# A gated MLP by seven block products in place of eight, with its inner features and residual kept in DRAM between its two halves

## The chip, the cores and the metric

The kernel runs on one core of one Trainium2 chip. Its time is device microseconds of one launch. Below, PE is TensorE (the matmul engine), PEld its weight loads, DVE is VectorE, ACT ScalarE, POOL GpSimd, and SP SyncE, which here only issues DMAs. SBUF is the on-chip memory, PSUM the memory that matmuls write and accumulate in, DRAM the chip's large memory.

## The reference, cut to what matters

Two transformer blocks run one after the other on 1024 tokens of 1024 features in float32. The change concerns the end of the first block: the second norm, the gated MLP with 2816 inner features, and the residual.

```
h = h + m @ w_o                                  # output of the mixer
hn = rms_norm(h, norm2_g)
gate, up = jnp.split(hn @ w_gate_up, 2, axis=-1) # w_gate_up [1024, 2 * 2816]
h = h + (jax.nn.silu(gate) * up) @ w_down        # w_down [2816, 1024]
x = rms_norm(h, final_g)                         # goes into the second block
```

Every float32 product is made of three passes: a matrix X is split into a high part hi(X), rounded to the format that PE multiplies in one pass, and a low part lo(X) = X - hi(X); then X @ Y = hi hi + hi lo + lo hi. So each product of 128 x 128 by 128 x 512 is three matmuls, and each operand costs one copy (ACT) and one subtraction.

## The kernel before, in words

The program is one stream with an order written out by hand: each engine gets its instructions in the order of the Python text, and waits only on semaphores. Tiles come from pools with a fixed number of buffers; a tile that takes over a buffer waits until the last reader of the old one is done. `Side` objects (class Side) are generators whose steps are put between the matmuls of the main stream; `tick` pays them out by an estimate of matmul time.

`Weights` streams the weights: SP loads a raw unit (`wraw`, 3 buffers), ACT makes the high part, POOL the low part (`whi`, `wlo`, 4 buffers each), two units ahead of use. PSUM has 6 banks named `mm` and 2 named `ax`, 128 x 512 each.

In the stage "wo" (line 1047) eight row tiles of h are loaded from x by ACT's queue (L1051), and `add_rows` adds the mixer's output, four column blocks of 256: first columns 0 and 1 for all rows, then the memory of the second block (`mem_steps`, `mem_kv`), then columns 2 and 3 for rows 0 to 3 and for rows 4 to 7. `norm2_steps` norms the first four row tiles beside the matmuls of the last four.

In the stage "mlp" (line 1164) POOL first fills a small table `G` of relative biases (L1175, 32 tiny instructions into an `ev` tile) and stores it 128-fold to DRAM (L1179). Then the normed rows are turned (`n2T`, `to_cols`) into nh, nl: features on partitions, 1024 tokens along the row. For each of 22 tiles of 128 inner features, `gate_up` makes the gate and the up product (8 blocks of K, three matmuls each, two halves of 512 tokens), Silu on ACT, the product of the two on DVE, and the high and low part of the inner feature (`acth`, `actl`). After each group of two or four tiles `down_unit` multiplies them by the rows of w_down and adds the PSUM sum to h in SBUF (L1206); so h gathers six partial sums, and the down product lies between the gate and up products. At the end `final_steps` norm h twice, rows 0 to 3 beside the last down products, rows 4 to 7 beside the first products of the stage "z", which turns rows 0 to 3 first.

Of the kernel before, what the change touches and what calls it, by code (L numbers as in the profile page):

```python
# [58 lines left out]
class Weights:  # L59
    """Streams weights in the order of use: DMA ahead, then exact high and low parts."""  # L60
# [21 lines left out]
    def split_to(self, n, low=None):  # L82
        nc = self.nc
        while self.ns < min(n, len(self.plan)):
# [27 lines left out]
def build(tc, A, out, dbg=None, stop=None):  # L112
# [85 lines left out]
    order = []                      # ("gu", tile) and ("dn", group), as they run
    for gi, (f0, nf) in enumerate(ff_groups):
        for f in range(f0, f0 + nf):  # L200
            order.append(("gu", f))
            if gi and f == f0:
                order.append(("dn", gi - 1))
    order.append(("dn", len(ff_groups) - 1))
    for kind, a in order:
        if kind == "gu":            # gate and up columns of one hidden tile share a unit
            for k0 in (0, 4):
                plan.append(("gu", [cols(wgu, a * 128, 128, k0), cols(wgu, DFF + a * 128, 128, k0)],
                             4, 256))
        else:  # L210
            f0, nf = ff_groups[a]
            for j in range(2):
                for k0 in range(0, nf, 2):
                    plan.append(("dn", cols(wdn, 512 * j, 512, f0 + k0, 2), 2, 512))
# [1471 lines left out]
```

## Time and profile before

| | |
|---|---|
| median of 3 runs | 2272.94 us (2271.72 to 2275.72) |
| the profiled execution: span from first to last instruction | 2270.9 us |
| PE busy | 2225.0 us, 98% |
| PEld busy | 1932.2 us, 85% |
| DVE busy | 1099.9 us, 48% |
| POOL busy | 704.1 us, 31% |
| ACT busy | 676.8 us, 30% |
| mean granted TensorE clock | 0.996 of 2.4 GHz |
| stage "wo" to the first turn of "mlp" | about 985 to 1085 us |
| gated MLP with the down product | about 1085 to 1834 us |

The profile is one execution; all its times are microseconds from the start of the span unless marked ns. A row of the timeline gives start, duration, engine, line, operation, the tile written and the tiles read, and in brackets the idle time before it and what ended that. The duration of a matmul overlaps with the next one, so the spacing of starts is what a matmul costs, not its duration. A row of the groups by line gives count, busy time and the mean of one in ns. A line of the stretches gives, for each engine, busy time and instruction count, then the granted clock, the share of the 16 DMA engines, and GB/s.

### The profile page before, as it was taken

The page shows a single profiled execution, that of the slowest core. Times are in us where ns is not written, and L with a number is a line of the kernel's source. Part 1 is how long each engine was busy: PE and PEld are TensorE (multiplying, and loading weights), DVE is VectorE, ACT ScalarE, POOL GpSimd, SP SyncE. Part 2 cuts the span into 40 slices and gives each one's busy share as a digit, 9 for nine tenths or more (in the row PEclk, how much of TensorE's full clock was granted, in tenths as well). Part 3 has the DMA queues.
Part 4 walks back from the last instruction along what each step waited for, and adds up shares of the span by engine and source line. Part 5 has one row for each costly group of instructions (what it writes and reads, how often), then busy time and mean ns, then how long its engine had stood idle before and what let it go on. Part 6 is the DMA issues. An engine that isn't in the chain of part 4 may idle for free.

```text
span 2270.9 us, 30698 instructions
## 1 busy us (share of the span) xinstructions
PE 2225.0 (98%) x12299; PEld 1932.2 (85%) x12299; DVE 1099.9 (48%) x2327; ACT 676.8 (30%) x1290; POOL 704.1 (31%) x581
## 2 busy tenths in 40 slices
PE   7999999999999999999799999999999999999998
PEld 7789888998888888899788888888888899988998
DVE  6688899888893887332320110101011170831724
ACT  4573211111122876212311112021211252322631
POOL 0213322325542311643243223232322212671121
PEclk9999999999999999999999999999999999999999
DMA  4212122113320000451221111111111132110014
GB/s 145 70 66 75 61 75 70 56 38 112 111 75 25 15 1 22 155 186 60 48 84 40 44 56 38 56 38 56 47 47 56 38 112 71 48 57 19 1 60 146
DMA packets 131950, 146.25 MB, mean 64 GB/s; under 512 B 11200, under 2 KB 112292, under 8 KB 131808
## 3 DMA queue, kind: packets, MB, share of 16 engines
q1 hardware_dynamic: 117600, 103.56, 14.8%
q0 software_dynamic: 8800, 27.54, 3.5%
q10 hardware_dynamic: 5408, 13.20, 1.5%
q8 instruction: 96, 1.57, 0.3%
q14 instruction: 46, 0.38, 0.1%
HBM read 122.48 MB, written 21.76 MB: 64 GB/s over the span
## 4 chain that ended last, share of the span: by engine, by line
PE 88%; DVE 5%; issue 3%; DMA 2%; ACT 1%; POOL 1%; ACTq 0%; DVEq 0%; SPq 0%; POOLq 0%
PE mm L293 26%; PE mm L295 26%; PE mm L294 25%; PE mm L966 2%; PE ax L293 2%; DMA gd<-ev 1%; PE ax L295 1%; PE ax L294 1%; PE ax L1569 1%; PE mm L1511 1%; PE mm L347 1%; DVE scores L575 1%; PE mm L1547 1%; DVE av L1373 1%; PE mm L569 0%
## 5 line engine op out<-in xcount | busy, mean ns | idle before, releaser
L91 POOL TENSOR_TENSOR wlo<-wraw,whi 128x1024 fp32r<-128x1024 f32 (+1 forms) x174 | 416.8, 2415 | 699.0 <-ACT whi L90 679.5
L293 PE MATMUL mm<-nh,whi 128*128 128x512 f32 (+1 forms) x736 | 282.6, 384 | 0.0
L295 PE MATMUL mm<-nh,wlo 128*128 128x512 f32 (+1 forms) x736 | 281.4, 382 | 0.0
L294 PE MATMUL mm<-nl,whi 128*128 128x512 f32 (+1 forms) x736 | 278.8, 379 | 0.0
L90 ACT ACTIVATE whi<-wraw 128x1024 fp32r<-128x1024 f32 (+1 forms) x176 | 178.8, 1050 | 311.3 <-issue 176.9
L295 PE MATMUL mm<-xh,wlo 128*128 128x512 f32 (+2 forms) x736 | 269.9, 367 | 0.0
L294 PE MATMUL mm<-xl,whi 128*128 128x512 f32 (+2 forms) x736 | 269.5, 366 | 0.0
L293 PE MATMUL mm<-xh,whi 128*128 128x512 f32 (+2 forms) x736 | 269.0, 365 | 0.0
L1191 DVE TENSOR_TENSOR ev<-mm,ev 128x512 f32<-128x512 f32 (+1 forms) x46 | 30.7, 668 | 450.3 <-PE mm L295 428.0
L618 DVE MAX8 m<-scores 128x8 f32<-128x272 f32 (+6 forms) x224 | 188.8, 843 | 6.4 <-POOL scores L580 0.2
L620 DVE MATCH_REPLACE8 scores<-m,scores 128x272 f32<-128x272 f32 (+6 forms) x224 | 185.0, 826 | 0.0
L322 POOL TENSOR_TENSOR actl<-ev,acth 128x512 fp32r<-128x512 f32 (+1 forms) x46 | 57.4, 1248 | 356.5 <-ACT acth L1193 356.5
L295 PEld LDWEIGHTS mm<-nh,wlo 128*128 128x128 f32 x736 | 138.2, 188 | 29.2
L294 PEld LDWEIGHTS mm<-nl,whi 128*128 128x128 f32 x736 | 138.1, 188 | 28.3
L293 PEld LDWEIGHTS mm<-nh,whi 128*128 128x128 f32 x736 | 138.3, 188 | 25.4
L294 PEld LDWEIGHTS mm<-xl,whi 128*128 128x128 f32 x736 | 138.5, 188 | 20.5
L293 PEld LDWEIGHTS mm<-xh,whi 128*128 128x128 f32 x736 | 138.3, 188 | 20.3
L295 PEld LDWEIGHTS mm<-xh,wlo 128*128 128x128 f32 x736 | 138.3, 188 | 19.6
L1206 DVE TENSOR_TENSOR h<-mm,h 128x512 f32<-128x512 f32 x96 | 66.3, 692 | 163.5 <-PE mm L295 163.5
L293 PE MATMUL mm<-whi,acth 128*128 128x512 f32 (+1 forms) x368 | 143.7, 391 | 0.0
L295 PE MATMUL mm<-whi,actl 128*128 128x512 f32 (+1 forms) x368 | 143.7, 391 | 0.0
L294 PE MATMUL mm<-wlo,acth 128*128 128x512 f32 (+1 forms) x368 | 143.7, 390 | 0.0
(320 smaller groups left out, 4833.8 us busy)
## 6 DMA issues: line engine op xcount, KB each, us to landing
wraw<-in_w_in_dram SPq DMA_DIRECT2D x68, 512.0 KB, 3.6
wraw<-in_w_gate_up_dram SPq DMA_DIRECT2D x88, 256.0 KB, 3.3
wraw<-in_w_down_dram SPq DMA_DIRECT2D x22, 512.0 KB, 3.6
mpart<-ev POOLq DMA_DIRECT2D x32, 256.0 KB, 2.3
ev<-mpart POOLq DMA_DIRECT2D x32, 256.0 KB, 3.7
xr<-in_x_dram SPq DMA_DIRECT2D x8, 512.0 KB, 6.6
g1d<-ev ACTq DMA_DIRECT2D x16, 256.0 KB, 2.0
wraw<-in_w_b_dram SPq DMA_DIRECT2D x8, 512.0 KB, 3.3
```

What stands on the lines that cost most here:

```text
L90: nc.scalar.activation(hi[:, :nk * w], r, AF.Copy)
L91: (low or nc.gpsimd).tensor_tensor(lo[:, :nk * w], r, hi[:, :nk * w].bitcast(F32), op=ALU.subtract)
L293: nc.tensor.matmul(o, sh, mh, start=start, stop=False)
L294: nc.tensor.matmul(o, sh, ml, start=False, stop=False)
L295: nc.tensor.matmul(o, sl, mh, start=False, stop=stop)
L322: (eng or nc.gpsimd).tensor_tensor(out_lo, src, hi.bitcast(F32), op=ALU.subtract)
L347: nc.tensor.transpose(tp[:, k * 128:k * 128 + P], r[:, kk * 128:(kk + 1) * 128], ident[:P, :P])
L618: nc.vector.max(m8, s)
L620: nc.vector.match_replace(out=s, in_to_replace=m8, in_values=s, imm_value=TAKEN)
L966: nc.tensor.transpose(tp[:P, h * 128:(h + 1) * 128], lgs[h][:, k0:k0 + P], ident)
L1191: nc.vector.tensor_tensor(g, ou, g, op=ALU.mult)
L1206: nc.vector.tensor_tensor(hs, o, hs, op=ALU.add)
```

## The change

The product of two matrices, each cut into 2 x 2 blocks, takes eight block products. The changed kernel takes seven, with the sums of blocks by Strassen and Winograd (numbered 1 to 7 in the code), for the gate, the up and the down product alike.

For gate and up, the turned rows are cut into two halves of tokens and two halves of K, and seven operands `TM[1]` to `TM[7]` are made once: 1 and 2 are blocks, the others differences of the normed rows, taken before the turn (`turn4`, through the two `ax` banks). A unit is 256 columns of gate or up; per unit DVE makes three sums of weight blocks and later a fourth (`gu_sums`, `gu_prep`), ACT and POOL split each of the seven weight operands, seven products of 12 matmuls run in the order 1, 6, 2, 5, 7, 3, 4 in four banks, and `gu_out`, `block` add the results up; POOL multiplies by the gate. Products 2, 3 and 4 add on to the banks of 1, 5 and 7 after those have been read. At each pair of units POOL makes the seven left operands of the down product (`hidden_sums`), and SP stores them to DRAM (`hd`).

The residual h is stored to DRAM (`hres`) after the mixer and loaded again at the down product. That starts when all inner features are done: seven products over 11 pairs of inner tiles, all of K summed in PSUM, in the order 1, 7, 2, 4, 5, 6, 3; each step loads one operand of the inner features (`ra`) and one or two blocks of w_down, makes the sum for products 7, 4 and 5 on DVE, and splits both operands: ACT copies, POOL's low part for the weights, DVE's for the inner features. Steps are prepared three ahead. The last three steps of each product go row tile by row tile, and `dn_out` adds the result to the blocks of h that take it.

Also moved: `G` is made at the start of "wo" into a tile of its own, the keys and values of the memory go through DRAM, rows 4 to 7 are final before rows 0 to 3, and the high and low weight parts share one ring of eight (`wpart`).

```diff
+    def raw_tile(self):
+        return self.pool.tile([128, 1024], F32, name="wraw", bufs=3)
+    def part_tile(self):
+        return self.pool.tile([128, 1024], F32R, name="wpart", bufs=8)
...
+    ht = {}
+    for t0, c in ((4, 1), (0, 0), (4, 0), (0, 1)):
+        for t in range(t0, t0 + 4):
+            ht[t, c] = hb_tile()
+            nc.scalar.dma_start(ht[t, c], x[t * 128:(t + 1) * 128, 512 * c:512 * c + 512])
...
+    def turn4(r, th, tl, c0):
+        tp = ax_tile()
+        for k in range(4):
+            nc.tensor.transpose(tp[:, k * 128:k * 128 + 128], r[:, k * 128:(k + 1) * 128], ident)
+        tv = tp.rearrange("p (k t) -> p k t", k=4)
+        hs = th[:, :, c0:c0 + 128]
+        nc.scalar.activation(hs, tv, AF.Copy)
+        nc.vector.tensor_tensor(tl[:, :, c0:c0 + 128], tv, hs.bitcast(F32), op=ALU.subtract)
...
+        if turns:
+            for p, c in ((1, 0), (2, 1)):
+                TM[p] = [tb_tile().rearrange("p (k t) -> p k t", k=4) for _ in range(2)]
+                for t in ts:
+                    turn4(ht[t, c], *TM[p], 128 * t)
+                    yield 1.3
...
+    relT = work.tile([4, 32], F32, name="relT")
+    G = tb_tile(F32)[:4, :384]
+    nc.scalar.dma_start(relT, A["rel_bias_2"].rearrange("b h -> h b"))
...
+    def gu_sums(u):
+        r0, r1 = gu_raw[u]
+        f1, f2 = slice(0, 128), slice(128, 256)
+        s1, s2, s3 = gu_sum[u] = [hb_tile().rearrange("p (k c) -> p k c", k=4) for _ in range(3)]
+        nc.vector.tensor_tensor(s1, r0[:, :, f2], r1[:, :, f2], op=ALU.add)
+        nc.vector.tensor_tensor(s2, s1, r0[:, :, f1], op=ALU.subtract)
+        nc.vector.tensor_tensor(s3, r0[:, :, f1], r0[:, :, f2], op=ALU.subtract)
...
+    n2a = Side(norm2_steps(range(4), True))
     for t in range(4, 8):
         add_rows(mh, ml, wo[2], t, 2)
+    gu_sums(0)
+    for n in range(4):
+        gu_prep(n)
...
+    for _ in norm2_steps(range(4, 8)):
+        pass
+    for t in range(4):
+        a, b = ht[t, 0], ht[t + 4, 0]
+        nc.gpsimd.tensor_tensor(a, b, a, op=ALU.subtract)
+        nc.vector.tensor_tensor(b, ht[t + 4, 1], b, op=ALU.subtract)
...
+    def hidden_sums(u):
+        pr = gu_units[u][1]
+        g = acc.pop(u - 1)
+        acc.pop(u)
+        a11, a12, a21, a22 = g[0, 0], g[1, 0], g[0, 1], g[1, 1]
+        s3, s2, s4 = (hb_tile() for _ in range(3))
+        nc.gpsimd.tensor_tensor(s3, a11, a21, op=ALU.subtract)
+        nc.gpsimd.tensor_tensor(a21, a21, a22, op=ALU.add)
+        nc.gpsimd.tensor_tensor(s2, a21, a11, op=ALU.subtract)
+        nc.gpsimd.tensor_tensor(s4, a12, s2, op=ALU.subtract)
+        for p, t in ((1, a11), (2, a12), (4, a22), (7, s3), (5, a21), (6, s2), (3, s4)):
+            store(p, pr, t)
...
+    gu_step(0)
+    gu_mm(1)
+    for t in range(4):
+        turn4(ht[t + 4, 1], *TM[3], 128 * t)
+    for t in range(4):
+        nc.vector.tensor_tensor(ht[t + 4, 1], ht[t + 4, 1], ht[t, 0], op=ALU.subtract)
+    for t in range(4):
+        nc.gpsimd.tensor_tensor(ht[t, 1], ht[t, 1], ht[t + 4, 1], op=ALU.subtract)
+    gu_step(2)
+    gu_mm(3)
+    for t in range(4):
+        turn4(ht[t + 4, 1], *TM[6], 128 * t)
...
+    for f in later:
+        f()
...
+        if p == 7:
+            nc.vector.tensor_tensor(t, rb[:, :512], rb[:, 512:], op=ALU.subtract)
+        elif p == 4:
+            nc.vector.tensor_tensor(t, t, rb[:, :512], op=ALU.add)
+            nc.vector.tensor_tensor(rb[:, :512], rb[:, 512:], t, op=ALU.subtract)
+        elif p == 5:
+            nc.vector.tensor_tensor(rb[:, :512], rb[:, :512], rb[:, 512:], op=ALU.subtract)
+        src = t if p in (6, 7) else rb[:, :512]
+        ops = []
+        for which, (tile_, x_) in enumerate(((W.part_tile(), src),
+                                             (dnp.tile([128, 1024], F32R, name="pa", bufs=6), ra))):
+            nc.scalar.activation(tile_[:, :512], x_, AF.Copy)
+            lo_of(tile_[:, 512:], x_, tile_[:, :512], nc.vector if which else nc.gpsimd)
```

The order of instructions, at three places. First ACT, from the mixer's output to the start of the MLP. Before (junk is the square for the norm, nh the turned rows, whi the weights' high parts):

```order
L326 ACTIVATE junk,ss<-h 128x1024 x4
L90 ACTIVATE whi<-wraw 128x1024 x2
L1168 DMA relT<-in_rel_bias_dram 4x32x1
L351 ACTIVATE nh<-mm 128x4x128 x8
L90 ACTIVATE whi<-wraw 128x1024 x2
L326 ACTIVATE junk,ss<-h 128x1024 x4
L1190 ACT_TABLE_LOAD
L1190 ACTIVATE ev<-mm 128x256
```

Now (hb are half rows of h, tb the operands 1 and 2, th_10079 operand 3, th_10081 operand 6; L1327 copies product 1 out of its bank):

```order
L317 ACTIVATE junk,ss<-hb 128x512 x8
L1214 ACTIVATE wpart<-wraw 128x512 x4
L1069 ACTIVATE tb<-ax 128x4x128 x8
L317 ACTIVATE junk,ss<-hb 128x512 x8
L1327 ACTIVATE ev<-mm 128x512
L1069 ACTIVATE th_10079<-ax 128x4x128 x4
L1327 ACTIVATE ev<-mm 128x512
L1069 ACTIVATE th_10081<-ax 128x4x128 x4
L1214 ACTIVATE wpart<-hb 128x512
L1275 ACT_TABLE_LOAD
```

The four weight splits now stand ahead of the eight copies of turned rows, and the copy of the first product stands behind all eight squares of rows 4 to 7.

Second, SP where the gate and up products end. Before:

```order
L78 DMA wraw<-in_w_gate_up_dram 128x4x128 x16
L78 DMA wraw<-in_w_down_dram 128x2x512 x4
L78 DMA wraw<-in_w_gate_up_dram 128x4x128 x12
L78 DMA wraw<-in_w_down_dram 128x2x512 x4
L78 DMA wraw<-in_w_in_dram 128x4x256 x11
```

Now:

```order
L1184 DMA wraw<-in_w_gate_up_dram 128x4x256 x4
L1266 DMA hd<-hb 128x512 x14
L1418 DMA ra<-hd 128x512
L1425 DMA wraw<-in_w_down_dram 128x512
L1418 DMA ra<-hd 128x512
```

All stores of the last pair of units stand ahead of the first load of the down product.

Third, DVE in the down product. Before (L1206 adds a PSUM sum to h, L1191 is the gated product):

```order
L1191 TENSOR_TENSOR ev<-mm,ev 128x512 x8
L1206 TENSOR_TENSOR h<-mm,h 128x512 x16
L1191 TENSOR_TENSOR ev<-mm,ev 128x512 x6
L1206 TENSOR_TENSOR h<-mm,h 128x512 x8
L274 TENSOR_SCALAR rv<-ss 128x4
```

Now, in product 4 (L313 is the low part of an inner operand, L1438 and L1439 the sums of w_down's blocks, L1462 adds product 2 to h):

```order
L313 TENSOR_TENSOR pa<-ra,pa 128x512
L1462 TENSOR_TENSOR hh<-mm,hh 128x512 x4
L1438 TENSOR_TENSOR tt<-tt,wraw 128x512
L1439 TENSOR_TENSOR wraw<-wraw,tt 128x512
L313 TENSOR_TENSOR pa<-ra,pa 128x512
L1438 TENSOR_TENSOR tt<-tt,wraw 128x512
```

Where DVE only read PSUM sums, it now has two or three instructions per step that read both operands from SBUF, and the low part of one step stands ahead of the sums of the next.

## Rows read from the trace of the kernel before

**Rows 1.** Busy time by stretch: PE, PEld, DVE, ACT, POOL; clock, DMA share, GB/s.

```profile
1200.00:1400.00 200.00, 200.00 (x872) 163.41 (x871) 20.76 (x30) 35.27 (x47) 59.32 (x32) 1.00 0.15 45
```

**Rows 2.** Groups by line and shape, PE: count, busy us, mean ns.

```profile
L293 PE MATMUL mm<-nh,whi 128*128 128x512 f32 x672 | 264.5, 394 | 0.0
...
L293 PE MATMUL mm<-whi,acth 128*128 128x512 f32 x352 | 139.2, 396 | 0.0
...
L293 PE MATMUL mm<-nh,whi 128*128 128x256 f32 x64 | 18.1, 283 | 0.0
```

**Rows 3.** Timeline of PE at the start of the gated MLP.

```profile
1110.91 1.03 PE L347 MATMUL mm<-ident,actl 128*128 128x128 f32 x8
1123.14 3.68 PE L347 MATMUL mm<-ident,actl 128*128 128x128 f32 x16 [11.19 <-ACT ev L1190]
1127.13 1.29 PE L347 MATMUL mm<-ident,actl 128*128 128x128 f32 x8 [0.31 <-DVE nl L352]
1128.32 0.39 PE L293 MATMUL mm<-nh,whi 128*128 128x256 f32 x1
...
1139.62 0.28 PE L295 MATMUL mm<-nh,wlo 128*128 128x256 f32 x1
```

**Rows 4.** Timelines of ACT and POOL there.

```profile
1122.70 0.38 ACT L1190 ACTIVATE ev<-mm 128x256 f32<-128x256 f32 x1 [20.52 <-DMA gd<-ev]
...
1079.44 8.85 POOL L1175 TENSOR_SCALAR ev<-relT 4x1 f32<-4x1 f32 x32
```

**Rows 5.** Stretches of that stall, columns as in rows 1.

```profile
1111.00:1123.00 12.00, 0.95 (x9) 0.71 (x7) 0.00 (x0) 0.30 (x1) 0.00 (x0) 0.76 0.25 32
1123.00:1126.00 3.00, 2.86 (x14) 2.86 (x15) 1.12 (x2) 1.75 (x5) 0.78 (x2) 0.50 0.12 47
```

**Rows 6.** Timelines at the start of the mixer's output: ACT's queue, POOL, DVE.

```profile
984.95 3.85 ACTq L1051 DMA_DIRECT2D h<-in_x_dram  x8
...
989.98 2.40 POOL L91 TENSOR_TENSOR wlo<-wraw,whi 128x1024 fp32r<-128x1024 f32 x1 [1.99 <-ACT whi L90]
...
1006.04 0.42 DVE L1069 TENSOR_TENSOR h<-mm,h 128x256 f32<-128x256 f32 x1 [2.40 <-PE mm L295]
```

**Rows 7.** Stretches of the same place, columns as in rows 1.

```profile
985.00:995.00 10.00, 10.00 (x87) 10.00 (x86) 1.54 (x4) 2.58 (x3) 7.36 (x6) 1.00 0.86 323
995.00:1005.00 10.00, 10.00 (x87) 10.00 (x86) 1.44 (x4) 0.31 (x1) 0.82 (x2) 1.00 0.97 359
```

**Rows 8.** DMA issues by line: size of one, median us from issue to landing.

```profile
wraw<-in_w_gate_up_dram SPq DMA_DIRECT2D x88, 256.0 KB, 3.3
...
g1d<-ev ACTq DMA_DIRECT2D x16, 256.0 KB, 2.0
...
h<-in_x_dram ACTq DMA_DIRECT2D x8, 512.0 KB, 9.3
```

**Rows 9.** Groups by line and shape of POOL, ACT and DVE, columns as in rows 2.

```profile
L322 POOL TENSOR_TENSOR actl<-ev,acth 128x512 fp32r<-128x512 f32 x42 | 54.4, 1296 | 315.8 <-ACT acth L1193 315.8
...
L1193 ACT ACTIVATE acth<-ev 128x512 fp32r<-128x512 f32 x42 | 26.5, 632 | 233.4 <-DVE ev L1191 233.4
...
L1041 DVE TENSOR_TENSOR ev<-ev 128x512 f32<-128x512 f32 x16 | 18.3, 1143 | 3.2 <-DMA ev<-mpart 2.2
L322 DVE TENSOR_TENSOR ol<-q,oh 128x512 fp32r<-128x512 f32 x16 | 9.7, 685 | 0.7 <-ACT oh L1006 0.7
```

**Rows 10.** Timelines of ACT and DVE in a norm of four rows.

```profile
1093.68 0.19 ACT L326 ACTIVATION_READ_ACCUMULATOR junk<-h 128x1 f32 x1
...
1065.24 0.17 DVE L274 TENSOR_SCALAR rv<-ss 128x4 f32<-128x4 f32 x1 [1.28 <-ACT junk L326]
...
1067.43 0.16 DVE L289 SCALAR_TENSOR_TENSOR ry<-rt,ry 128x4 f32<-128x4 f32 x1
```

**Rows 11.** Timelines of POOL and DVE where both read SBUF.

```profile
964.52 4.74 POOL L91 TENSOR_TENSOR wlo<-wraw,whi 128x1024 fp32r<-128x1024 f32 x2
...
967.41 2.40 DVE L1041 TENSOR_TENSOR ev<-ev 128x512 f32<-128x512 f32 x1
```

More of the change, by code (lines that the diff above doesn't have):

```diff
@@ L195, in build @@
                 plan_cols("mkv", A["w_mem_kv_2"][0], 256 * jj)
-    ff_groups = [(0, 2), (2, 4), (6, 4), (10, 4), (14, 4), (18, 4)]
     wgu, wdn = A["w_gate_up"][0], A["w_down"][0]
[L198 to L214, printed above, removed]
+    n_first = len(plan)
     for j in range(4):
@@ L1079, in norm2_steps @@
+    TM = {}
+    def norm2_steps(ts, turns=False):
+        ss = [work.tile([128, 4], F32, name="ss", bufs=4) for _ in range(2)]
+        for i, t in enumerate(ts):
+            for c in range(2):
+                sumsq(ht[t, c], ss[c][:, i:i + 1])
+                nc.sync.dma_start(hres[t, :, 512 * c:512 * c + 512], ht[t, c])
+            yield 1.2
+        nc.vector.tensor_tensor(ss[0], ss[0], ss[1], op=ALU.add)
+        y = rstd_b(rstd_a(ss[0], k=4))
         yield 1.0
         for i, t in enumerate(ts):
-            hn[t] = ah(F32) if t < 4 else al(F32)
@@ L1093, in mem_steps @@
+    gd = dram.tile([4, 128, 384], F32, name="gd")
+    nc.gpsimd.dma_start(gd, G.unsqueeze(1).to_broadcast([4, 128, 384]))
     def mem_steps():
         ss = work.tile([128, 4], F32, name="ss", bufs=4)
-        for r, m in enumerate(mrows):
-            sumsq(m, ss[:, r:r + 1])
+        for r in range(2):
+            sumsq(mrows[:, r, :], ss[:, r:r + 1])
             yield 1.0
@@ L1212, in build @@
[L1212 to L1247 removed]
+    tmp_ = pool("tm", side="left")
@@ new lines, in gu_mm @@
+    def gu_mm(n):
+        u, p = gu_seq[n]
+        s = acc.setdefault(u, {})
+        bank = {1: "a", 2: "a", 6: "b", 5: "c", 3: "c", 7: "d", 4: "d"}[p]
+        first = p not in (2, 3, 4)
+        if first:
+            s[bank] = mm_tile()
+        o = s[bank]
+        hi, lo = gu_ops.pop(n)
+        th, tl = TM[p]
+        for k in range(4):
+            mm3(o, hi[:, k, :], lo[:, k, :], th[:, k, :], tl[:, k, :], first and k == 0, k == 3, not first)
+        for f in later:
+            f()
+        later.clear()
@@ new lines, in build @@
+    gu_sums(1)
+    gu_out(3)
+    for n in (5, 6, 7):
+        gu_prep(n)
+    gu_step(4)
+    for t in range(4):
+        turn4(ht[t, 0], *TM[5], 128 * t)
+    gu_step(5)
+    gu_prep(8)
+    for t in range(4):
+        turn4(ht[t + 4, 0], *TM[7], 128 * t)
+    gu_step(6)
+    gu_prep(9)
+    gu_step(7)
+    gu_prep(10)
+    for t in range(4):
+        turn4(ht[t, 1], *TM[4], 128 * t)
+    ahead = 11
+    for n in range(8, len(gu_seq)):
+        while ahead <= n + 6:
+            gu_prep(ahead)
+            ahead += 1
+            if ahead < len(gu_seq):
+                gu_load(gu_seq[ahead][0])
+        gu_step(n)
@@ new lines, in build @@
+    for f in later:
+        f()
+    later.clear()
+    close(hbp)
+    close(tmp_)
+    close(tbp)
+    MARK("down")
+    hpool = pool("h2", side="right")
+    h = hpool.tile([128, NT, D], F32, name="hh")
+    for t in range(NT):
+        nc.scalar.dma_start(h[:, t, :], hres[t])
+    hxp = pool("hx", side="right")
+    fg = hxp.tile([128, D], F32, name="fg")
+    pg2 = hxp.tile([128, D], F32, name="pg2")
+    nc.gpsimd.dma_start(fg, A["final_g"].rearrange("(a d) -> a d", a=1).to_broadcast([128, D]))
@@ L1294, in build @@
     hl = h2p.tile([128, 8, S], F32R, name="hl")
-    fa.drain()
-    for t in range(4):
+    fb.drain()
+    for t in range(4, 8):
         to_cols(h[:, t, :], hh, hl, t * 128)
```

388 lines of the change are left out of this document (236 added, 152 removed).

## The prediction

> **What bounds the kernel now.** I read the stretches first. In steady gate and up work [rows 1] PE is busy all 200 us while DVE, ACT and POOL have 21, 35 and 59 us of work: the stage is bound by matmuls, and everything else hides. The price of a matmul is not its mean duration of 394 to 396 ns [rows 2], since matmuls overlap, but the spacing of starts: 200 us / 872 = 0.2294 us for 512 columns [rows 1]; for 256 columns, 11.30 us between the first and the last of 96 starts [rows 3] / 95 = 0.119 us. Next I looked for the places where PE is idle. Near the change there is one, at the start of the MLP: PE waits 11.19 and then 0.31 us in the turns [rows 3], because the copy of a turned tile into an `ev` buffer waits 20.52 us for the store of G, which 32 tiny POOL instructions filled late [rows 4]. The granted clock is 0.76 over that stall and 0.50 of 2.4 GHz, the 1.2 GHz level, in the 3 us behind it [rows 5]: an idle PE costs its idle time and some slow time after.
>
> So matmuls taken out give their full price, as long as no new wait of PE opens. I therefore price the matmuls, then walk the order of every engine for new waits. All sums are against the profiled span, 2270.9 us; the runs' median, 2272.9, lies 2.0 above, and I add that at the end.
>
> **The products.** Gate and up have 2016 matmuls of 512 columns and 192 of 256 (three lines with 672 and 64 each, [rows 2]): 2016 x 0.2294 + 192 x 0.119 = 462.5 + 22.8 = 485.3 us. Now 22 units x 7 products x 12 = 1848 x 0.2294 = 423.9: -61.4. Down has 3 x 352 = 1056 matmuls [rows 2] and gets 7 x 11 x 4 x 3 = 924: -30.3. Together **-91.7**. Turns: 28 groups of four in place of 64 transposes, 48 more at 1.03 / 8 = 0.129 us [rows 3]: **+6.2**.
>
> The rate rests on [rows 1]. The Trainium skill (TensorE: Matmul & The Clock Gate, Back-to-back issue gap) gives some 131 ns for a sustained 512-column matmul; 300 fewer of 512 and 192 of half that width would then give only about 52 us, and by my other terms the time would rise to about 2301. The trace's spacing of 0.229 decides against it.
>
> **Is steady gate and up work still bound by PE?** A pair of units is 168 matmuls, 38.5 us. POOL has 21 instructions on half rows there (14 low parts, the gate, four hidden sums): at 1.27 to 1.3 us [rows 9] 27 us. DVE has eight sums with both operands in SBUF at 0.69 [rows 9] and some 16 reads of PSUM; ACT some 20 copies at 0.63. All fit with six steps of lead: nothing added.
>
> **G goes away from the MLP's start**: 11.2 + 0.3 idle [rows 3, 4] and the half-speed turns behind it, where 24 took about 5.0 us instead of 3.1, and a little before them: **-13.8**.
>
> **G comes back at the start of the mixer's output.** Its relT load now stands on ACT's queue behind 16 loads of x (4 MB as before, where eight took 3.85 us to issue [rows 6]), and DMA there runs at 323 to 359 GB/s with shares of 0.86 and 0.97 [rows 7]. 4 MB at that rate is 12 us and more, so relT lands at about 996 to 1003. Then POOL works 8.85 us [rows 4] and issues DMAs, and only then makes the low part of the weights of column 1, which before stood at 989.98 [rows 6]. It is ready at 1009 to 1015; PE needs it at about 1006 to 1007.6, when column 0 ends [rows 6]. **+7** (2.5 to 10.5).
>
> **Turns in the mixer's tail.** The four weight splits of unit 0 now stand ahead of the eight copies of turned rows on ACT. The fourth split needs a raw block whose buffer comes free only after the sums of unit 0, and which then takes 3.3 us to land [rows 8]; with two `ax` banks the third turn holds PE until the first copy is done. PE has slack of the same size: **+4.5** (0 to 6).
>
> **The MLP's start**, from the last addition of the mixer's output on. ACT does eight squares at 0.63 + 0.19 us [rows 9, 10] = 6.5 before it copies product 1, so product 2, which takes the same bank, waits 4 to 4.5 us. DVE then has the chain of small operations, 2.4 us [rows 10], eight norms at 0.69, and four subtractions that change places with four of POOL's at 1.27 [rows 9]. Only then can operand 3 be turned, two banks at a time. Chained, PE goes on about 25 us after the last addition and has 7.6 us of products until then: 17 idle. Operand 6's turns add 4.7 in the same way, operands 5, 7 and 4 another 4, and the 1.2 GHz level [rows 5] 2.5: **+28** (18 to 34).
>
> **From gate and up to down.** Before, the down product lay among the others and PE had no gap. Now, after the last product, DVE adds (0.69), POOL multiplies by the gate and makes four sums, 5 x 1.27: some 7.3 us to the last operand. SP's order puts all the stores ahead of the first load of the down product: the last store, then 0.5 us to issue, 3.3 to land (256 KB [rows 8]), ACT's copy 0.63, a low part 0.69 to 1.27: 14 us idle and 2 of half clock, **+16** (9 to 20). The stores' own landing (2.0 us [rows 8] in a store of that size) is in the upper end.
>
> **Down steps with sums on DVE.** A step is 12 matmuls, 2.75 us. In products 7, 5 and 4 it also needs on DVE one sum (two for 4) and the low part of the inner operand, both with two SBUF operands, and a low part on POOL in between: sum, ACT copy, POOL's low part, DVE's low part, next sum. Whether DVE and POOL run these beside each other is the largest question here. [Rows 9] has 0.685 us for such a DVE instruction with POOL idle, 1.143 for one beside POOL; [rows 11] shows why: while POOL did two low parts of 2.37 us, an addition of two SBUF tiles on DVE took 2.40, ending with POOL's. So I take turns as the rule: a chain of 0.69 + POOL's 1.27 + 0.69 and what lies between (ACT's copy 0.63, semaphores) is 3.4 us a step for products 7 and 5, 4.1 for 4. Against 2.75, over 11 steps and less what three steps of lead absorb: 3.7 + 10.1 + 9.9 = **+24** (0 to 45: all hidden, or ends that miss each other), with half clock in those waits **+4** (0 to 8). The other four products need 2.0 us a step or less: hidden.
>
> The Trainium skill (SBUF — State Buffer, SBUF: two separate sides) says the same against this change: a DVE instruction with two SBUF inputs and a GpSimd one that reads SBUF exclude each other for a whole instruction. The trace agrees (2.40 us for 0.69); without it the sum would be the first rival's below.
>
> **Product 3** has the norms of rows 4 to 7 beside its steps on ACT and DVE: **+4** (0 to 8). The start of stage "z" keeps its cover with the rows exchanged: 0. The DMA traffic added (hd, hres, w_down again, some 30 MB over 700 us) is small beside a stretch at 45 GB/s [rows 1] when 359 were moved elsewhere [rows 7].
>
> **Sum**: -91.7 + 6.2 - 13.8 + 7 + 4.5 + 28 + 16 + 24 + 4 + 4 = -11.8. Span 2259, time **2261 us**, faster by 0.5%. Nearly all of the 92 us of matmuls is given back in waits, so the sign hangs on the large ones.
>
> **The rivals.**
> First, the lead covers the down product (or POOL and DVE miss each other): the terms 24, 4 and 4 go, 2261 - 32 = 2229. For it: 1.143 us as the mean of the additions beside POOL [rows 9] is well under a whole turn, so many met no POOL instruction. Against: [rows 11], and here POOL's part lies between DVE's two in every step. Chance 0.24.
>
> Second, slower: the raw loads of the down product, not the engines, set its pace. The raw tiles of w_down have three buffers, and one is held from the load's issue until the step's low part is made. With a landing time L that is (L + 2.6) / 3 a step for products 7 and 5, (L + 3.3) / 3 for 4. At 3.3 us [rows 8] that is 2.0 to 2.2, hidden; but at the 9.3 of the x loads [rows 8] it is 4.0 and 4.2. Over these 33 steps the loss is about 11 L - 89, which at 9.3 is 14 us more than my 28: 2275; from L = 9.6 on, the change is slower than before by more than 0.2%; with three issues of 0.48 us [rows 6] before each landing (10.7) it gives 2290. For it: rows of one operand come from DRAM freshly written, in three loads a step. Against: traffic of about 0.75 MB in 3 us, 250 GB/s, lies below the 323 to 359 of [rows 7]. Chance 0.18.
>
> Third, the waits at the MLP's start, in the mixer's tail and at the border come out at their low ends, beside the first rival: 2229 - 10 - 7 - 4.5 = 2207. Chance 0.08.
>
> **Numbers.** My forecast has 0.50. Its own range, 2246 to 2276, comes from the half widths of its terms (3.5, 3, 8, 5, 8) added as independent ones, about 13, and a little more. The measurement can tell about 0.2% from no change, so the bounds are 2268.4 and 2277.5. Of the forecast's 0.50, 0.36 is faster, 0.11 the same, 0.03 slower; the first and third rival are faster (0.32); the second has 0.02 within and 0.16 above. Faster 0.68, same 0.13, slower 0.19. For 8 in 10 the range goes from 2222, which takes in the first rival, to 2287, which takes in most of the second.
>
> **What would show it.** Matmul counts of 1848 and 924, at a spacing of 0.229 in steady gate and up work; if it is more there, that term fails first. PE's idle time before the transposes of line 1066 and before lines 284 to 286 at the MLP's start (28 in sum); POOL's G and the wait of PE in column 1 of the mixer's output (7); the gap between the last gate and up matmul and the first of the down product (16 with the slow clock). In the down product, the period of steps: 3.4 us in products 7 and 5, 4.1 in 4, 2.75 elsewhere; L1436, L1438, L1439, L1441 and L313 on DVE at 1.2 us or more where POOL's L313 is beside them. If their duration is 0.69 and the period 2.75, the first rival holds; if DVE and ACT wait for DMAs instead, and `ra` or `wraw` lands in 9 us, the second. The forecast is wrong as a whole if PE is idle in a place not named here.

## The result, and the profile after

| | before | changed |
|---|---|---|
| median | 2273.3 us (4 runs) | 2313.5 us (4 runs, 2312.7 to 2315.6) |
| ratio | | 1.0181, interval 1.0167 to 1.0196 |
| span of the profiled execution | 2270.9 us | 2311.4 us |
| PE busy | 2225.0 us | 2177.3 us |
| mean granted TensorE clock | 0.996 | 0.973 |

The change made the kernel slower by 1.8%; the forecast was 2261 us, faster, in a range from 2222 to 2287. The matmuls were saved as forecast, by their count. The groups by line of the changed kernel, PE only, from 1140 to 1880 us (columns as in rows 2; two more lines stand for each of these):

```profile
L284 PE MATMUL mm<-th,wpart 128*128 128x512 f32 x440 | 171.9, 391 | 2.5 <-DVE hb L1277 1.3 <-ACT wpart L1214 1.2
L284 PE MATMUL mm<-wpart,pa 128*128 128x512 f32 x242 | 103.3, 427 | 22.8 <-ACT pa L1446 22.8
L284 PE MATMUL mm<-tb,wpart 128*128 128x512 f32 x176 | 71.4, 405 | 4.6 <-ACT ev L1327 4.6
```

With 66 more of the down product in the `ax` banks, that is 3 x (440 + 176) = 1848 and 3 x (242 + 66) = 924. The stretches of steady gate and up work, which answer to [rows 1]:

```profile
1200.00:1400.00 200.00, 198.68 (x866) 161.81 (x867) 80.63 (x103) 63.79 (x111) 151.36 (x111) 1.00 0.31 104
1400.00:1600.00 200.00, 200.00 (x871) 163.22 (x870) 73.83 (x94) 56.01 (x97) 141.28 (x103) 1.00 0.29 97
```

PE is full there, at the same spacing as before (200 / 871 = 0.2296 us), with POOL busy for 141 to 151 us in place of 59. The time is lost before this stage and behind it. The waits of PE, summed by what ended them, of the stretch 985 to 1200 us:

```profile
PE mm L1136 <- DVE tb L1131: 28.9, 2, 28.4
PE ax L1066 <- DVE tl L1070: 13.3, 5, 8.0
PE mm L285 <- POOL wpart L97: 10.0, 1, 10.0
PE ax L1066 <- DVE tb L1070: 7.2, 1, 7.2
PE mm L284 <- ACT ev L1327: 4.6, 2, 3.9
```

The first line is the largest, and no step of the prediction names it: PE waits 28.4 us in the turns of the second block's memory rows (L1136), for a norm on DVE. Followed back, the norm waits for squares on ACT, and these stand behind a weight copy that waits for a load. ACT and POOL there, from their timelines:

```profile
1002.13 8.85 POOL L1117 TENSOR_SCALAR tb<-relT 4x1 f32<-4x1 f32 x32 [15.03 <-DMA relT<-in_rel_bias_dram]
1011.28 1.15 POOL L1121 DMA_DIRECT2D gd<-tb  x1 [0.30 <-POOL tb L1117]
1012.46 4.67 POOL L97 TENSOR_TENSOR wpart<-wraw,wpart 128x1024 fp32r<-128x1024 f32 x2
...
1048.16 1.06 ACT L96 ACTIVATE wpart<-wraw 128x1024 fp32r<-128x1024 f32 x1 [43.81 <-DMA wraw<-in_w_mem_kv_dram]
1049.13 1.04 ACT L317 ACTIVATE junk<-tb 128x1024 bf16<-128x1024 f32 x1
```

The DMA issues of 985 to 1060 us, first of the changed kernel, then of before (columns as in rows 8), and a stretch of the wait (columns as in rows 1):

```profile
wraw<-in_w_mem_kv_dram SPq DMA_DIRECT2D x3, 512.0 KB, 32.3
...
gd<-tb POOLq DMA_DIRECT2D x1, 768.0 KB, 35.1
```

```profile
wraw<-in_w_mem_kv_dram SPq DMA_DIRECT2D x3, 512.0 KB, 3.7
```

```profile
1025.00:1050.00 25.00, 1.57 (x14) 1.36 (x12) 0.00 (x0) 1.84 (x2) 0.70 (x1) 0.62 0.26 44
```

The 128-fold store of G (`gd`) lands 35.1 us after its issue. The memory's weights, issued behind it, land after 32.3 us in place of 3.7. From 1025 to 1050 the DMA engines are busy for 0.26 of their time. What the queue of these loads (q1, SP's) moves from 1014 to 1026 us, and then from 1026 to 1046 (packets, MB, share of 16 engines):

```profile
q1 hardware_dynamic: 1188, 1.18, 29.1%
```

```profile
q1 hardware_dynamic: 95, 0.10, 1.4%
```

The three loads are 1.57 MB. Three quarters of that are moved at once, and most of the last quarter only when the store ends: the loads go through the quarter of the engines that the store keeps busy, too.

The whole difference, stage by stage. The loss of a stage is its length on PE less its matmuls at 0.2294 us and its turns at 0.129, so the first two rows are counts at these prices. The row of G's stall is the loss of the whole MLP before, 1085.11 to 1836.63 (256 columns at 0.119). The mixer's output is held against its length before, 983.23 to 1085.11, which had no loss:

| term | predicted | measured |
|---|---|---|
| matmuls | -91.7 | -91.7 |
| turns | +6.2 | +6.2 |
| stall of G at the MLP's start, gone | -13.8 | -15.7 |
| mixer's output: G, memory, turns (981.95 to 1140.81) | +11.5 | +52.9 |
| the MLP's start (1140.81 to 1605.6) | +28 | +30.6 |
| border to down: gap, and product 1 behind it | +16 | 13.2 + 3.7 |
| products 7, 4, 5 | +28 | 4.2 + 10.8 + 7.2 |
| products 2 and 6 | 0 | 0.5 + 0.5 |
| product 3 | +4 | +17.9 |
| sum | -11.8 | +40.3 |

The spans differ by 40.5. Of the 52 us between the sums, 41 lie in the mixer's output and 14 in product 3.

### The profile page after: what moved, and what is told of

It reads as the page before. It is cut to its first block, busy times and chain, and to the rows that moved or that the text cites. A ratio compares the mean times of both kernels' runs of the same rounds, so it can differ in the third digit from the quotient of the medians.

```text
span 2311.4 us, 31362 instructions
## 1 busy us (share of the span) xinstructions
PE 2177.3 (94%) x11855; PEld 1876.5 (81%) x11855; DVE 1344.1 (58%) x2569; ACT 783.9 (34%) x1538; POOL 935.8 (40%) x789
## 5 line engine op out<-in xcount | busy, mean ns | idle before, releaser
L97 POOL TENSOR_TENSOR wpart<-wraw,wpart 128x1024 fp32r<-128x1024 f32 (+1 forms) x108 | 259.9, 2424 | 532.8 <-ACT wpart L96 513.2
L286 PE MATMUL mm<-xh,wpart 128*128 128x512 f32 (+2 forms) x736 | 269.9, 367 | 0.0
L285 PE MATMUL mm<-xl,wpart 128*128 128x512 f32 (+2 forms) x736 | 269.5, 366 | 0.0
L284 PE MATMUL mm<-xh,wpart 128*128 128x512 f32 (+2 forms) x736 | 269.0, 365 | 0.0
L313 POOL TENSOR_TENSOR wpart<-wraw,wpart 128x512 fp32r<-128x512 f32 x121 | 168.1, 1396 | 140.1 <-ACT wpart L1446 82.3
L286 PE MATMUL mm<-th,wpart 128*128 128x512 f32 x440 | 174.2, 396 | 0.6 <-POOL wpart L313 0.6
L284 PE MATMUL mm<-th,wpart 128*128 128x512 f32 x440 | 171.9, 391 | 2.5 <-DVE hb L1277 1.3
L285 PE MATMUL mm<-tl,wpart 128*128 128x512 f32 x440 | 172.9, 393 | 0.0
L284 PEld LDWEIGHTS mm<-xh,wpart 128*128 128x128 f32 x736 | 138.3, 188 | 20.4
L286 PEld LDWEIGHTS mm<-xh,wpart 128*128 128x128 f32 x736 | 138.3, 188 | 19.5
L313 DVE TENSOR_TENSOR pa<-ra,pa 128x512 fp32r<-128x512 f32 x77 | 99.4, 1308 | 84.3 <-ACT pa L1446 77.0
L284 PE MATMUL mm<-wpart,hh 128*128 128x256 f32 x512 | 142.0, 277 | 1.7 <-ACT ev L1666 1.7
L286 PE MATMUL mm<-wpart,hl 128*128 128x256 f32 x512 | 141.6, 277 | 0.0
L285 PE MATMUL mm<-wpart,hh 128*128 128x256 f32 x512 | 141.6, 277 | 0.0
L313 POOL TENSOR_TENSOR wpart<-hb,wpart 128x512 fp32r<-128x512 f32 x88 | 113.8, 1296 | 55.6 <-ACT wpart L1214 39.0
L284 PE MATMUL mm<-wpart,pa 128*128 128x512 f32 x242 | 103.3, 427 | 22.8 <-ACT pa L1446 22.8
L286 PE MATMUL mm<-wpart,pa 128*128 128x512 f32 x242 | 103.2, 427 | 6.2 <-DVE pa L313 5.9
L285 PE MATMUL mm<-wpart,pa 128*128 128x512 f32 x242 | 103.1, 426 | 1.5 <-POOL wpart L313 1.3
```

The source lines that it names most:

```text
L97: (low or nc.gpsimd).tensor_tensor(lo[:, :nk * w], r, hi[:, :nk * w].bitcast(F32), op=ALU.subtract)
L284: nc.tensor.matmul(o, sh, mh, start=start, stop=False, skip_group_check=more)
L285: nc.tensor.matmul(o, sh, ml, start=False, stop=False, skip_group_check=more)
L286: nc.tensor.matmul(o, sl, mh, start=False, stop=stop, skip_group_check=more)
L313: (eng or nc.gpsimd).tensor_tensor(out_lo, src, hi.bitcast(F32), op=ALU.subtract)
```

## Experiments

Theory A for the first four runs: the store of G blocks the loads behind it. Its rival B: POOL, late with G, frees the raw buffers late, and that delays the memory's weights. The times of before beside these runs were 2272.3 to 2273.3 us.

### G alone, put into the kernel before

The block that makes and stores G, moved to the start of the mixer's output in the kernel before, into the tile that later holds a gain:

```diff
     # cut: the whole block that fills and stores G moves
-    G = ev()[:4, :384]        # at the start of stage "mlp"
...
+    G = pg2[:4, :384]         # ahead of mem_steps
```

> The kernel before with this one part of the change alone: G is made and stored at the start of the mixer's output, in a tile that nothing else needs then. Theory A: 10 us wait for column 1, 28 us in the memory's turns and some 6 of half clock come, 15.7 us of the stall at the MLP's start go: 2273 + 44 - 16 = about 2301. If the waits come from something else in the changed kernel (its sixteen loads of x, its stores of the residual), only the POOL's 10 come: 2273 + 10 - 16 = about 2267.

Measured: 2302.6 us, ratio 1.0133 (1.0118 to 1.0148). PE's waits there:

```profile
PE mm L1121 <- DVE actl L1116: 29.7, 2, 29.3
PE mm L294 <- POOL wlo L91: 7.7, 1, 7.7
```

This one edit, without any of the new products, costs 29.9 us against the kernel before beside it (2272.7), and both waits appear; the stall at the MLP's start is gone in this run, so the new place costs more than that. The cause is in G's place.

### The store, the order and the load of G, one at a time

> The changed kernel with one edit: POOL stores G once (4 x 384) to DRAM, and a second DMA copies it 128-fold from DRAM to DRAM. POOL's work and its place stay. Theory A (the 128-fold store out of 4 SBUF partitions keeps a quarter of the DMA engines busy for 35 us, and the memory weights issued behind it land 32 us late): the copy lands within some 10 us, PE's 28.4 us wait in the memory's turns falls under 3, the 10.0 us wait for column 1's low part stays; 2313 - 29 - 4 of half clock = about 2280. Theory B (POOL's late low parts free the raw buffers late, and that delays the memory weights): nothing changes, 2313.

```diff
-    nc.gpsimd.dma_start(gd, G.unsqueeze(1).to_broadcast([4, 128, 384]))
+    g0 = dram.tile([4, 384], F32, name="g0")
+    nc.gpsimd.dma_start(g0, G)
+    nc.gpsimd.dma_start(gd, g0.unsqueeze(1).to_broadcast([4, 128, 384]))
```

Measured: 2294.1 us, 14 above what was expected. The copy lands 11.8 us after its issue, the memory's weights after 10.3, and PE's wait is 7.2 us in all, not under 3; the wait for column 1 is 11.5. The direction is theory A's, the copy is slower than I thought.

> The changed kernel with the 128-fold store of G issued behind the memory's keys and values; G itself is made where it was. Theory A: the 28.4 us wait goes and the 10.0 us wait stays, as in the run with the spread store; the store then lands some 35 us later, beside the loads of the output and gate weights and ahead of the turns that take over G's buffer, which may cost 0 to 20: 2276 to 2300. Theory B: 2313.

```diff
-    nc.gpsimd.dma_start(gd, G.unsqueeze(1).to_broadcast([4, 128, 384]))
...
         if j == 1:
             memside.drain()
             mem_kv()
+            nc.gpsimd.dma_start(gd, G.unsqueeze(1).to_broadcast([4, 128, 384]))
```

Measured: 2287.2 us, in theory A's range. The memory's weights land in 5.9 us, the wait is 1.4, and that for column 1 stays (8.2). The store still takes 35.3 us and now costs a few us in the turns: a wait for a norm (L330) that is 1.2 us in the changed kernel is 5.7.

> The changed kernel with relT loaded ahead of the sixteen loads of x. Both theories: POOL makes G from about 990 us and the 10.0 us wait goes. Theory A: the store is issued at about 998, lands at about 1033, and PE, which now comes to the memory's turns at about 1012, still waits some 20 us: 2313 - 12 - 6 = about 2295. Theory B: both waits go, about 2272.

```diff
+    nc.scalar.dma_start(relT, A["rel_bias_2"].rearrange("b h -> h b"))
     ht = {}
     for t0, c in ((4, 1), (0, 0), (4, 0), (0, 1)):
...
-    nc.scalar.dma_start(relT, A["rel_bias_2"].rearrange("b h -> h b"))
```

Measured: 2300.9 us, 6 above theory A's. POOL makes G from 988.7 us and the wait for column 1 is gone, but PE still waits 27.4 us for the memory's rows (I had some 20: PE comes to them that much earlier, and the weights still land 32.2 us after their issue). Theory B, which had both waits vanish, falls here.

### Why the store is slow

> The changed kernel with G spread to 128 partitions before the large store: 4 x 384 to DRAM, four small loads that put each head's row on 32 partitions, and then the store of the same 768 KB in the same rows of 1536 bytes, from 128 partitions, four times each. Theory A (the store is slow because it leaves SBUF by 4 partitions): it lands in under 8 us in place of 35, the memory weights land in under 12, and PE's 28.4 us wait falls under 8; about 2290. Theory B (512 rows of 1536 bytes, or the writing to this DRAM tile, are slow from anywhere in SBUF): it still lands some 35 us after its issue and the wait stays near 28: 2315 or a little more, since the small DMAs ahead of it add time.

```diff
+    G, GB = GT[:4, :384], GT[:, 512:896]
...
-    nc.gpsimd.dma_start(gd, G.unsqueeze(1).to_broadcast([4, 128, 384]))
+    g0 = dram.tile([4, 384], F32, name="g0")
+    nc.gpsimd.dma_start(g0, G)
+    for hh_ in range(4):
+        nc.gpsimd.dma_start(GB[32 * hh_:32 * hh_ + 32, :], g0[hh_:hh_ + 1, :].to_broadcast([32, 384]))
+    nc.gpsimd.dma_start(gd.rearrange("h (j r) c -> (h j) r c", r=4), GB.unsqueeze(1).to_broadcast([128, 4, 384]))
```

Measured: 2287.2 us. The DMA issues and the waits of PE in this run:

```profile
wraw<-in_w_mem_kv_dram SPq DMA_DIRECT2D x3, 512.0 KB, 6.4
...
gd<-tb POOLq DMA_DIRECT2D x1, 768.0 KB, 4.0
```

```profile
PE mm L285 <- POOL wpart L97: 16.0, 1, 16.0
PE mm L1141 <- DVE tb L1136: 1.0, 2, 0.6
```

The same 768 KB in the same rows of 1536 bytes, from 128 partitions in place of 4, land in 4.0 us in place of 35.1, and the 28.4 us wait is 0.6. (PE waits 6 us longer for column 1, since POOL now issues five more DMAs and waits for them.) The Trainium skill (DMA: Bandwidth & Descriptors, Why a DMA increments its semaphore by 16 and not by 1) says that a DMA is shared out over the largest number of engines, up to 16, that divides the slowest dimension of both its sides. That dimension is 4 for this store, and the busy share of 0.26 agrees; so do the 4.0 us with 128 there. The copy from DRAM, whose slowest dimension is 4 too, took 11.8 us, which that rule alone does not give. In its run the stretch before the weights come (columns as in rows 1) has the same share, but far more bytes:

```profile
1018.00:1020.00 2.00, 2.00 (x10) 2.00 (x11) 0.00 (x0) 0.00 (x0) 2.00 (x1) 0.50 0.26 108
```

In the changed kernel the engines move 29 GB/s at a share of 0.25 (1035 to 1045 us). So a quarter of the engines is not the whole reason. The rest goes with reading G out of 4 partitions of SBUF; how, no run here shows.

### Both costs of G away

> The changed kernel with both costs of G taken away and the rest of the change kept: relT is loaded ahead of x, G goes to DRAM once (4 x 384), and the 128-fold copy from there is issued behind the memory's keys and values. Theory A (late POOL and the slow store are all that the move of G costs): the waits of 10.0 and 28.4 us and some 5 us of half clock go, 2313 - 44 = about 2269, near the kernel before. If the copy from DRAM gets into the way of the weights that are loaded beside it: up to 2280.

Edits of the three runs above together: relT first, G to DRAM once, the copy behind `mem_kv`. Measured: 2269.9 us, ratio 0.9983 (0.9974 to 0.9993). The stretch of the mixer's output, first of the changed kernel, then of this run (columns as in rows 1):

```profile
985.00:1060.00 75.00, 36.12 (x269) 35.45 (x268) 8.63 (x27) 7.26 (x10) 20.64 (x43) 0.73 0.41 115
```

```profile
985.00:1060.00 75.00, 75.00 (x647) 75.00 (x646) 17.31 (x45) 21.40 (x36) 35.76 (x50) 1.00 0.52 176
```

PE is busy throughout and the clock stays at its 2.4 GHz level. The place and the store of G cost the change 43.6 us, and without them it is 0.2% faster than before.

### DVE and POOL in the down product

> The changed kernel with the weights' low parts of products 7, 4 and 5 on DVE in place of POOL, and the inner feature split first. Theory A (DVE and POOL take turns, which makes the step 3.25, 4.39 and 3.42 us): DVE's low part falls from 1.37 to 0.69 us, the steps cost 2.8 us, and of the loss of 22 us in these products some 18 go: about 2295. Theory B (the raw blocks set the pace): the steps keep their period, 2313.

```diff
+        dve = p in (7, 4, 5)
+        for which in ((1, 0) if dve else (0, 1)):
...
-            lo_of(tile_[:, 512:], x_, tile_[:, :512], nc.vector if which else nc.gpsimd)
+            lo_of(tile_[:, 512:], x_, tile_[:, :512], nc.vector if which or dve else nc.gpsimd)
```

First the changed kernel, product 4, the timelines of DVE and POOL:

```profile
1705.58 1.36 DVE L313 TENSOR_TENSOR pa<-ra,pa 128x512 fp32r<-128x512 f32 x1 [1.22 <-ACT pa L1446]
1706.87 0.68 DVE L1438 TENSOR_TENSOR tt<-tt,wraw 128x512 f32<-128x512 f32 x1
1707.99 0.69 DVE L1439 TENSOR_TENSOR wraw<-wraw,tt 128x512 f32<-128x512 f32 x1 [0.44 <-issue]
1709.90 1.36 DVE L313 TENSOR_TENSOR pa<-ra,pa 128x512 fp32r<-128x512 f32 x1 [1.22 <-ACT pa L1446]
```

```profile
1705.10 1.29 POOL L313 TENSOR_TENSOR wpart<-wraw,wpart 128x512 fp32r<-128x512 f32 x1 [3.76 <-ACT wpart L1446]
1709.43 1.29 POOL L313 TENSOR_TENSOR wpart<-wraw,wpart 128x512 fp32r<-128x512 f32 x1 [3.03 <-ACT wpart L1446]
```

POOL's low part ends at 1705.10 + 1.29 = 1706.39; DVE's, begun at 1705.58, runs on to 1706.94, some 0.55 us behind POOL's end, and needs 1.36 us in all. This step is 1709.90 - 1705.58 = 4.32 us long; the median in product 4 is 3.97. Now the run with both low parts on DVE, the same line (L313) from 1640 to 1780 us (shortest, median and longest duration in ns):

```profile
L313 DVE TENSOR_TENSOR pa<-ra,pa x50: 677/686/1795, 1640.2 to 1779.0; 128x512 fp32r<-128x512 f32 x50
L313 DVE TENSOR_TENSOR wpart<-wraw,wpart x22: 684/692/693, 1704.1 to 1766.7; 128x512 fp32r<-128x512 f32 x22
```

Measured: 2294.8 us, ratio 1.0098 (1.0081 to 1.0116): 18.7 us faster than the changed kernel. Products 7, 4 and 5 now lose 0.5 us each, and DVE, with more work, is faster. The steps waited for engines, not for loads: the raw blocks came by the same queue with the same buffers. The edit changes three things at once: POOL no longer works beside DVE, the weights' low part takes 0.68 us in place of 1.29, and the inner operand is split first. What each of them gives was not separated.

### Product 3

In the changed kernel, the sixth to eighth step of product 3 are 5.80, 5.87 and 7.99 us long on PE, and the last three take 14.49 together. ACT, then DVE, from their timelines there:

```profile
1832.11 0.62 ACT L1446 ACTIVATE pa<-ra 128x512 fp32r<-128x512 f32 x1
...
1838.63 1.06 ACT L317 ACTIVATE junk<-hh 128x1024 bf16<-128x1024 f32 x1
...
1840.20 0.61 ACT L1446 ACTIVATE pa<-ra 128x512 fp32r<-128x512 f32 x1
```

```profile
1835.75 2.47 DVE L330 SCALAR_TENSOR_TENSOR hh<-hh,ry,fg 128x1024 f32<-128x1024 f32 x2
1840.85 1.42 DVE L313 TENSOR_TENSOR pa<-ra,pa 128x512 fp32r<-128x512 f32 x1 [2.63 <-ACT pa L1446]
1842.19 2.47 DVE L330 SCALAR_TENSOR_TENSOR hh<-hh,ry,fg 128x1024 f32<-128x1024 f32 x2
1847.29 1.41 DVE L313 TENSOR_TENSOR pa<-ra,pa 128x512 fp32r<-128x512 f32 x1 [2.62 <-ACT pa L1446]
```

ACT's squares (L317) wait for DVE's norms (L330), ACT's copy of the next step stands behind the squares, and DVE's low part (L313) waits for that copy, with the next norms behind it: a round of 1847.29 - 1840.85 = 6.44 us, where a step of PE is 2.8.

> The changed kernel without the norms beside product 3: all of rows 4 to 7's final norms run behind it. Any theory that makes the norms the cause: product 3 loses 0.5 to 2 us in place of 17.9, and PE then waits some 20 us for the norms, so about 2313 + 4 = 2317. If the loads or POOL's low parts are the cause, product 3 still loses 10 or more and the time is 2325 or more.

```diff
-        if p == 6 and len(grp) > 1:
-            fb = Side(final_steps(range(4, 8)))
+    fb = Side(final_steps(range(4, 8)))      # behind the loop over the products
```

Measured: 2313.6 us (2 runs). All steps of product 3 take 2.80 us, and PE then waits for the norms, 14 us and not the expected 20:

```profile
1872.94 6.20 PE L338 MATMUL mm<-ident,hh 128*128 128x128 f32 x32 [13.99 <-DVE hh L330]
```

So the norms are the cause, and they cost as much beside product 3 as behind it: as ordered, the cover that the change gives them is worth nothing.

> The changed kernel with one edit in the final norm: the square (and the store of the row, which ACT also issues) of a row tile stands two places behind its norm in the order, in place of right behind it. Theory A (in product 3 ACT's copies of the next step stand behind squares that wait for DVE's norms, and DVE's low parts behind those copies, so the two engines go round in 6.4 us per step): product 3's loss of 17.9 us falls to some 5, 2313 - 12 = about 2301. Theory B (DVE has too much work in product 3, or POOL's low parts hold it up): the loss stays within 3 us, 2311 to 2314.

```diff
-            norm_b(y[:, i:i + 1], h[:, t, :], fg, h[:, t, :])
-            nc.scalar.dma_start(x1d[t], h[:, t, :])
-            sumsq(h[:, t, :], s2[:, i:i + 1])
+            if i < 4:
+                norm_b(y[:, i:i + 1], h[:, ts[i], :], fg, h[:, ts[i], :])
+            if i > 1:     # i now runs to 5
+                nc.scalar.dma_start(x1d[ts[i - 2]], h[:, ts[i - 2], :])
+                sumsq(h[:, ts[i - 2], :], s2[:, i - 2:i - 1])
```

Measured: 2310.4 us, a miss: 3 us in place of 12. The first eight steps now take 2.80 us, as the theory wants, but the loss has moved into the last three steps, which PE takes together (product 3: 13.8 us lost in place of 17.9). Two waits make it:

```profile
1857.27 0.80 PE L286 MATMUL mm<-wpart,pa 128*128 128x512 f32 x1 [5.57 <-DVE pa L313]
...
1862.36 0.79 PE L286 MATMUL mm<-wpart,pa 128*128 128x512 f32 x1 [3.45 <-DVE pa L313]
```

The last low parts stand on DVE behind the second norm's small operations and its products.

> The changed kernel with the later squares of the run before, and in products 6 and 3 five steps of lead in place of three (eight buffers for inner operands). With the squares out of the way the last three steps of product 3 still waited 9 us in all for low parts that stand on DVE behind the second norm's small operations and its products with the gain, which POOL's 2.8 us low parts of the next weights stretch. Theory A (their place in the order is the cause): two steps more of lead put them ahead of these, product 3's loss falls from 17.9 (13.8 with the squares alone) to 3 to 6, about 2300. Theory B (the amount of DVE's work there): 2310.

```diff
-        while ready <= grp[-1] + 3 and ready < len(dn_seq):
+        while ready <= grp[-1] + (5 if p in (6, 3) else 3) and ready < len(dn_seq):
```

with eight `pa` buffers in place of six and the squares as in the run above. Measured: 2304.9 us for about 2300; product 3 loses 7.3 us, just over the 3 to 6 expected, so place in the order is most of it; one wait of 4.6 us for the last low part stays. What shares in that I did not separate.

### The MLP's start and the border

> The changed kernel with the eight subtractions of normed rows written behind the turns of operand 3, which does not need them. Theory A (POOL's four subtractions stretch DVE's eight norms from 5.5 to 8.4 us, and DVE's four stand ahead of the low parts that the third turn waits for): the 8.0 us wait falls to about 1.5, less what operand 6 is then late by: 2313 - 5 = about 2308. Theory B (the squares and the small operations set the end): 2313.

Edit: the loop with the eight subtractions stands behind the four `turn4` of operand 3. Measured: 2311.6 us (2 runs); the wait of 8.0 us is 4.6, where 1.5 was forecast, and the difference in time is within what two runs can tell. The eight norms on DVE, first in the changed kernel, then in this run, and the first of POOL's four subtractions in this run:

```profile
1149.76 8.44 DVE L330 SCALAR_TENSOR_TENSOR hb<-hb,ry,ev 128x512 f32<-128x512 f32 x8
```

```profile
1151.85 8.43 DVE L330 SCALAR_TENSOR_TENSOR hb<-hb,ry,ev 128x512 f32<-128x512 f32 x8
```

```profile
1152.74 1.66 POOL L1351 TENSOR_TENSOR hb<-hb 128x512 f32<-128x512 f32 x1 [21.18 <-DVE hb L330]
```

The edit moved DVE's four subtractions behind the turns, and that took 3.4 us off the wait. POOL's four did not move in time: POOL has nothing to do in the turns, and so still subtracts beside the norms, which stay as long. The first half of theory A, that POOL stretches them, is not tested by this run.

> The changed kernel with the last multiplication by the gate and the last four hidden sums on DVE in place of POOL: 5 x 0.69 = 3.5 us in place of 6.5 behind the last addition. Theory A (that chain, then the stores, then the loads make the gap): the gap of 13.2 us falls by 3, about 2310. Theory B (the loads of the residual and the weights that run there make it): it stays, 2313.

Edit: `nc.vector` for `nc.gpsimd` in the last multiplication by the gate and the last `hidden_sums`. Measured: 2309.3 us (2 runs); the gap before the down product is 10.16 us in place of 13.15, as forecast.

### All edits together

> All edits together that take a wait away (G, the low parts of products 7, 4 and 5 on DVE, later squares and five steps of lead in product 3, subtractions behind the turns of operand 3, the last sums on DVE). If the terms add up: 2313 - 44 - 18 - 11 - 2 - 4 = about 2234, faster than the kernel before by 1.7%.

Measured: 2232.0 us, ratio 0.9816 (0.9802 to 0.9831), faster than both kernels; the terms add up to 2 us. What is left of the change's waits is 26 us from the mixer's tail to the MLP's start, the gap of 10.15, and a loss of 7 in product 3.

## Why the prediction was wrong, by its own steps

**The products and the turns**: right. The spacing of starts carried over [rows 1] and gave 0.2296; only in the down product it was 2.80 / 12 = 0.233, 3.6 us in all.

**G goes away from the MLP's start**: right, -15.7 for -13.8. (What waited for G's buffer there was the output of Silu, L1190, not a copy of a turned tile.)

**G comes back at the start of the mixer's output**: the step that failed. It priced POOL's lateness well (a wait of 10.0 us for 7, within 2.5 to 10.5) and counted of G's DMAs only their issue. Their landing was in the trace: ACT waited 20.52 us for G's store [rows 4], and over that stall DMA was busy 0.25 at 32 GB/s [rows 5]. I read those rows for what waited on the buffer and for the clock, and asked neither why a store takes so long nor which loads would be queued behind it in its new place. The trace of the kernel before even had the price of both, in its DMA issues of 1080 to 1130 us (columns as in rows 8):

```profile
gd<-ev POOLq DMA_DIRECT2D x1, 768.0 KB, 34.0
wraw<-in_w_gate_up_dram SPq DMA_DIRECT2D x2, 256.0 KB, 29.7
```

The weights behind the store were 29.7 us late there, too, but PE did not wait for them; in the new place the memory's weights, which PE's next work hung on, were issued 4 to 10 us behind the store. That made 28.9 us of waits. With the 10.0 for column 1, the 7.2 of the turns and 6.8 us that are no wait (the clock was at its 1.2 GHz level, 0.50, from 1016 to 1020, behind the first wait), the stage lost 52.9 instead of 11.5.

**Turns in the mixer's tail**: +4.5, with 6 as the upper end; PE waited 7.2. **The MLP's start**: right in mechanism and size (28, measured 30.6). PE waited first for ACT's copy behind the squares (3.9) and then for operand 3's low parts behind norms and subtractions (8.0); DVE's eight norms took 8.4 us where the prediction has 8 x 0.69 = 5.5; that POOL's subtractions beside them did that is likely, but no run took them away. **Border**: 16, measured 13.2 and a slow product 1.

**Down steps with sums on DVE**: right in mechanism, 22.2 for 28. From one low part on DVE to the next it is 3.26, 3.97 and 3.18 us (medians of products 7, 4 and 5), forecast at 3.4, 4.1 and 3.4. As steps are prepared three ahead, PE's own stay at 2.80 us for the first eight in products 7 and 5 and the first seven in product 4; the loss falls nearly all on the last three, which PE takes together. The taking of turns in [rows 11] was the rule here, and it was gone when the low parts went to DVE. (In [rows 11] DVE ends at 967.41 + 2.40 = 969.81, 0.55 us behind POOL's 969.26, and not with it.) The first rival falls by that, and the second, by loads, too: they landed in 3.5 us (w_down) and 3.9 (`ra`). (Its 11 L - 89 is the loss beyond my 28, and not the loss itself; the times that it gives are right.)

**Product 3**: the term was mis-sized, 17.9 for 4 (0 to 8). I summed the norms' work and did not write out the order of ACT and DVE there, as I had done for the MLP's start; the round between the two engines is visible in the order alone.

The range failed because its upper end held only the rivals I had named. None of the three has the cause that decided, and of the slower side's 0.19, 0.16 was given to a mechanism that did not occur.

## What to carry to other kernels

When a block is moved, move its DMAs' whole flight with it: look up how long each takes to land, why, and which loads will be issued in that time. A DMA out of four partitions can hold up every load behind it (32.3 us in place of 3.7 here); spread it over all partitions first. Where two in-order engines feed each other beside a matmul loop, write out their order for one step and sum the round: if it is longer than the step, work "beside" the loop is not hidden.

## What the runs showed of the hardware that I had not expected

- A store of 768 KB from 4 partitions of SBUF took 34.0 us in the kernel before and 35.0 to 35.5 in every run that has it in another place, 4.0 from 128 partitions, and 11.8 to 12.7 as a copy from DRAM with the same shape. Loads on another queue, issued behind the slow store, moved three quarters of their bytes at once and landed when it did.
- Beside POOL's subtractions DVE's small instructions took longer, too: in product 3 a `TENSOR_SCALAR` of 128 x 4 took 1.24 us beside POOL's low part, against 0.17 in [rows 10], and both rows below ended within 0.03 us of one of POOL's:

```profile
1848.62 1.24 DVE L264 TENSOR_SCALAR rv<-ss 128x4 f32<-128x4 f32 x1
1849.89 1.20 DVE L265 TENSOR_SCALAR ri<-rv 128x4 int32<-128x4 int32 x1
```

- DVE and POOL did not always end together: DVE's low part took 1.36 us and ended 0.55 us behind POOL's, so it seems to have done most of its own work after POOL's end.
